# Sorted expert pairs visited in the order of ranks 0, 3, 1, 4, 2, 5, the lighter ranks cut to 64 slots, the rare pass's condition moved to the second pair

## The chip, the cores and the metric

The kernel runs on one core of a Trainium2 chip. The metric is the device time of one execution in microseconds; below it is given as the median of a few executions, and beside it stands one execution that was taken with the hardware profiler. PE is TensorE, DVE is VectorE, ACT is ScalarE, POOL is GpSimd, SP is the engine that issues the transfers.

## The reference

Two networks follow each other on 256 tokens of width 1024: a block with two feed-forward parts and a mixer, and then two layers that each end in a mixture of experts. The change touches only the mixture:

```python
def grouped_moe(h, w_router, router_bias, w_gate, w_up, w_down):
    scores = jax.nn.sigmoid((t @ w_router).astype(jnp.float32))
    # best 1 of 4 groups by the sum of its two best experts, then the best 2 experts in it
    combine = (one_hot(eidx, N_EXPERTS) * w[..., None]).sum(-2)
    for e in range(N_EXPERTS):                       # 16 experts of width 512
        he = jax.nn.silu(t @ w_gate[e]) * (t @ w_up[e])
        y = y + combine[:, e:e + 1] * (he @ w_down[e])
```

Every token goes to two of the 16 experts, so an expert sees some 32 tokens on average, and how many it really sees depends on the data.

## The kernel before, in words

`moe` (L1741) runs once per layer, after `route` has found the experts. It walks over eight **pairs** of experts. A pair owns twelve weight tiles of 1 MB: eight of gate and up, four of down. Sixteen tiles fit on the chip at a time, and `pump` (L316 and after) issues a tile's transfer on SP as soon as the tile 16 places earlier has been released: eight places free after a pair's gate and up (`self.release(8)`), four after its down. Each transfer raises one of eight semaphores in turn and first waits for the transfer eight places before it, so at most eight are under way.

Two pairs (`FIXED = 2`) stand in the order of the weights. The other six are sorted by `sort` (L1406): the count of a pair is that of its fuller expert, `pick` is a matrix that says which pair stands at which place, and SP reads the sorted numbers into registers, from which the later transfers take their addresses. Places p = 2 to 7 so hold ranks 0 to 5, fullest first.

How much a pair computes depends on its count `cv`, by branches that are taken on the chip:

- every pair: gate and up for slots 0 to 31 (`gate_up`, L1582, on `x(0)`), the activation (`swiglu`), down, and the scatter of the pair before it into the result `xT`;
- `cv > 32`: gate and up for slots 32 to 63 (in `more_gate_up`, L1626), and the longer `down2` (L1611) for both;
- `cv > 64`: slots 64 to 95 as well. Their tokens are gathered by `over_pick` and `over_turn`, ahead of knowing whether they are needed, in the `cv > 32` branch. `downs` then has a further branch (L1652), and `more_scatter` (L1754) adds their rows behind the next pair;
- `cv > 96`: the **rare pass** (`rest`, L1728), one condition for the whole layer, `top > NORMAL`. It stands at p = 3 (`RARE_AT`), and its body, which fetches weights once more into the pages that `gather` also uses, is skipped here.

At odd p below 7 a `gather` (L1466) collects the tokens of the next two pairs: PE multiplies one-hot rows by the hidden state into PSUM, and ACT and DVE copy the result into two pages, from which the next pair's `x(0)` is read.

A pair below is **light** when it runs slots 0 to 31 alone, **middle** with the `cv > 32` branch, **heavy** with the `cv > 64` branch.

Of the kernel before, what the change touches and what calls it, by code (L numbers as in the profile page):

```python
# [11 lines left out]
F32 = mybir.dt.float32  # L12
# [4 lines left out]
ALU = mybir.AluOpType  # L17
AX = mybir.AxisListType
ENG = mybir.EngineType

P = 128
S = 256
# [169 lines left out]
def _consts():  # L192
    t = np.arange(P)
    iota = np.broadcast_to(np.arange(1, 257, dtype=np.float32), (P, 256))
    tri = (t[:, None] < t[None, :]).astype(np.float32)
    i4 = np.arange(4)
    before = np.broadcast_to((i4[None, :] < i4[:, None]).astype(np.float32).reshape(1, 16), (P, 16))
    ip = np.arange(NPAIR - 2)
    ahead = np.broadcast_to((ip[None, :] < ip[:, None]).astype(np.float32).reshape(1, -1), (P, ip.size ** 2))
    inv = np.broadcast_to((10000.0 ** (-np.arange(16) / 16)).astype(np.float32), (P, 16))  # L200
    seg = np.broadcast_to((np.arange(256) % 64 != 0).astype(np.float32), (P, 256))
    parts = [("ident", np.eye(P, dtype=np.float32)), ("iota", iota), ("tri", tri), ("before", before),
             ("ahead", ahead), ("inv", inv), ("seg", seg)]
    off = 0
    for n, a in parts:
        _CO[n] = (off, a.shape[1])
        off += a.shape[1]
    return np.ascontiguousarray(np.concatenate([a for _, a in parts], axis=1).astype(np.float32))


FIXED = 2
NDYN = NPAIR - FIXED
NORMAL = 96
LAST = 224
RARE_AT = 3
LEVELS = (64, 32, 16, 8, 4, 2, 1, 0)


# [52 lines left out]
class K:  # L271
# [1137 lines left out]
    def sort(self, cnt, comb):  # L1409
        v = self.nc.vector  # L1410
        n = NDYN
        w0 = self.taken
        t = lambda w, nm, dt=F32: self.rt.tile([P, w], dt, name=self.uid(nm), tag=nm)
        sq = lambda x: x[:, :].rearrange("p (i j) -> p i j", i=n)
        c = cnt[:, FIXED:NPAIR]
        a, b = c.unsqueeze(1).to_broadcast([P, n, n]), c.unsqueeze(2).to_broadcast([P, n, n])
        gt, ge, tm = t(n * n, "ogt"), t(n * n, "oge"), t(2 * n * n, "otm")
        v.tensor_tensor(sq(gt), a, b, ALU.is_gt)
        v.tensor_tensor(sq(ge), a, b, ALU.is_ge)
        v.copy_predicated(gt, self.ahd, ge)  # L1420
        rk = t(n, "ork")
        v.tensor_reduce(rk, sq(gt), AX.X, ALU.add)
        io = self.co("iota")[:, 0:n]
        v.scalar_tensor_tensor(sq(ge), rk[:, :].unsqueeze(1).to_broadcast([P, n, n]), 1.0,
                               io.unsqueeze(2).to_broadcast([P, n, n]), ALU.add, ALU.is_equal)
        pick = sq(ge)
        out = []
        for src, nm in ((self.posm, "posp"), (comb, "comp")):
            dst = t(32, nm)
            for tt in range(2):  # L1430
                o = tt * 16
                v.tensor_copy(dst[:, o:o + 2 * FIXED], src[:, o:o + 2 * FIXED])
                tm4 = tm[:, :].rearrange("p (q e j) -> p q e j", q=n, e=2)
                dims = [P, n, 2, n]
                e2 = src[:, o + 2 * FIXED:o + 16].rearrange("p (j e) -> p e j", e=2)
                v.tensor_tensor(tm4, e2.unsqueeze(1).to_broadcast(dims), pick.unsqueeze(2).to_broadcast(dims), ALU.mult)
                v.tensor_reduce(dst[:, o + 2 * FIXED:o + 16], tm[:, :].rearrange("p (a b) -> p a b", b=n), AX.X, ALU.add)
            out.append(dst)
        self.posm, self.comb = out
        srt = t(2 * n + 1, "srt")  # L1440
        for k, src in enumerate((c, io)):
            v.tensor_tensor(sq(gt), src.unsqueeze(1).to_broadcast([P, n, n]), pick, ALU.mult)
            v.tensor_reduce(srt[:, k * n:(k + 1) * n], sq(gt), AX.X, ALU.add)
        v.tensor_scalar(srt[:, n:2 * n], srt[:, n:2 * n], 12.0, float(w0 + 12 * (FIXED - 1)), ALU.mult, ALU.add)
        v.tensor_reduce(srt[:, 2 * n:], cnt, AX.X, ALU.max)
        self.srti = t(2 * n + 1, "srti", I32)
        v.tensor_copy(self.srti, srt)
        for q in range(n):
            r = self.nc.values_load(self.srti[0:1, n + q:n + q + 1], engines=[ENG.SP], min_val=w0,
                                    max_val=w0 + 12 * NPAIR - 12)  # L1450
            for i in range(12):
                self.dyn[w0 + 12 * (FIXED + q) + i] = r + i
# [173 lines left out]
    def more_gate_up(self, p, cv, gu, x1, tg, h2, pw):  # L1626
        nc, tc = self.nc, self.tc
        ox = self.rt.tile([P, 2, S], F32, name=self.uid("ox"), tag="ox")
        with tc.If(cv > 32):
            xs = self.over_pick(p, 64)  # L1630
            ps = self.mm()
            last = self.gate_up(ps, gu, x1, range(4))
            last = self.chain(last, self.over_turn(xs, ox))
            self.weigh(pw, p, 0, 1)
            last = self.gate_up(ps, gu, x1, range(4, 8), last)
            nc.scalar.activation(tg, ps, AF.Copy)
            with tc.issue_after(last.ins):
                with tc.If(cv > 64):
                    ps = self.mm()
                    self.gate_up(ps, gu, lambda k, e: ox[:, k // 4, (k % 4) * 64 + 32 * e:(k % 4) * 64 + 32 * e + 32])  # L1640
                    t2 = self.sq512()
                    nc.scalar.activation(t2, ps, AF.Copy)
                    self.swiglu(t2, h2)

    def downs(self, p, cv, dn, hT, y, w, more):
        nc, tc = self.nc, self.tc
        pss = [self.mm() for _ in range(2)]
        with tc.If(cv > 32) as c:
            last = self.down2(pss, dn, hT[0], hT[1])
            self.y_page(y, pss, w)  # L1650
            with tc.issue_after(last.ins):
                with tc.If(cv > 64):  # L1652
                    w2, st2 = more[2:]
                    pw = self.tmp.tile([P, 2, P], F32, name=self.uid("pw"), tag="t1")
                    ps2 = [self.acc() for _ in range(2)]
                    last = self.down(ps2, dn, hT[2])
                    with tc.issue_after(last.ins):
                        self.weigh(pw, p, 64)
                        self.slot_w(pw, w2, st2)
                    self.y_page(more[:2], ps2, w2)  # L1660
        with c.Else():
            self.down(pss, dn, hT[0])
            self.y_page(y, pss, w)

    def rare(self, p, e, lo, w0):
        nc = self.nc
# [61 lines left out]
    def rest(self, w0):  # L1728
        engs = [ENG.PE, ENG.Activation, ENG.DVE, ENG.SP]
        load = lambda i: self.count(i, engs)  # L1730
        top = self.nc.values_load(self.srti[0:1, 2 * NDYN:2 * NDYN + 1], engines=engs, min_val=0, max_val=S)
        with self.tc.If(top > NORMAL):
            for p in range(NPAIR):
                cv = load(p)
                for lo in (NORMAL, LAST):
                    with self.tc.If(cv > lo):
                        for e in range(2):
                            self.rare(p, e, lo, w0)

    def moe(self, l, ahead):  # L1740
        nc = self.nc  # L1741
        v = nc.vector
        self.l = l
        self.route(l)
        engs = [ENG.PE, ENG.Activation, ENG.DVE]
        w0 = self.taken
        self.pump()
        tg = [self.rt.tile([P, 512], F32, name=self.uid("tg"), tag=f"tg{i}") for i in range(2)]
# [3 lines left out]
        more = [self.rt.tile([P, D], F32R, name=self.uid("y2"), tag=f"y2{i}") for i in range(2)]  # L1752
        more += self.slots("st2")

        def more_scatter():
            with self.tc.If(cvp > 64):
                self.scatter(more[0], more[1], more[3])

        for p in range(NPAIR):
            base = (p % 2) * P  # L1760
            pw = self.rt.tile([P, 2, P], F32, name=self.uid("pw"), tag="pw")
            self.weigh(pw, p, 0)
            gu = [[[self.get(nm) for _ in range(2)] for nm in ("w_gate_2", "w_up_2")] for _ in range(2)]
            x = lambda lvl: lambda k, e: xe[k // 4][:, (k % 4) * S + base + 64 * e + 32 * lvl:
                                                    (k % 4) * S + base + 64 * e + 32 * lvl + 32]
            hT = [self.rt.tile([P, S], F32, name=self.uid("hT"), tag=f"hT{i}") for i in range(3)]
            ps = self.mm()
            last = self.gate_up(ps, gu, x(0))
# [3 lines left out]
                self.more_gate_up(p, cv, gu, x(1), tg[1], hT[2], pw)  # L1772
            gu = None
            self.release(8)
            if p > 0:
                more_scatter()
            w, st = self.slots("sT", 2)
            self.slot_w(pw, w, st)
            last = None
            if prev is not None:  # L1780
                self.scatter(*prev, 0, 4)
            if p == RARE_AT:
                self.rest(w0)
            for i in range(2):
                self.swiglu(tg[i], hT[i])
            if prev is not None:
                last = self.scatter(*prev, 4, 4, 512)
            if p % 2 == 1 and p < NPAIR - 1:
# [9 lines left out]
            prev, cvp = (y[0], y[1], st), cv  # L1798
            dn = None
            self.release(4)  # L1800
        more_scatter()
        if l == 1:
            self.final_diag()
        self.scatter(*prev)
# [208 lines left out]
```

## Time and profile before

| | us |
|---|---|
| median of 3 executions (1515.75 to 1520.26) | 1518.95 |
| the profiled execution's own time | 1516.88 |
| its span | 1515.1 |
| PE busy (share of the span) | 1373.0 (91%) |
| DVE busy | 971.5 (64%) |
| ACT busy | 683.5 (45%) |
| transfers of the weights' queue, as a share of 16 engines' span | 67.2% |

The page divides the span by engine. The two mixtures are the stretches from about 745 to 1018 us and from about 1255 to 1504 us. The rows below are read from there: a timeline row gives start, duration, engine, line, operation, tile written and tiles read, the count of instructions merged, and in brackets the idle time before it with what ended that. A window row gives busy time by engine, the clock that TensorE was granted (1.00 is 2.4 GHz, 0.50 is 1.2 GHz), the busy share of the DMA engines and what they moved.

### The profile page before, as it was taken

Reading aid. Unit: us, or ns where it says so; the run is one execution under the profiler, and the core shown is the slowest. Engines: PE = TensorE matmul, PEld = TensorE weight load, DVE = VectorE, ACT = ScalarE, POOL = GpSimd, SP = SyncE. Lnnn points to the kernel's source line nnn. Section 1 sums busy time; section 2 is a strip of 40 time slices with the busy share of each in tenths; the row PEclk is TensorE's granted clock in tenths of the full one; section 3 lists DMA queues with packets and bytes.
Section 4 is the critical chain, followed back from the end, with each engine's and each line's share of the span. In section 5 each row is a group of like instructions: output and inputs, shape, how many; then the busy total and the mean of one; then the engine's idle time right before and its main releaser. Section 6 shows DMA issues by size and latency. Waiting matters only on the chain. (4 is left out here: it accounts for less than half of the span.)

```text
span 1515.1 us, 27586 instructions
## 1 busy us (share of the span) xinstructions
PE 1373.0 (91%) x10666; PEld 1091.1 (72%) x10666; DVE 971.5 (64%) x2159; ACT 683.5 (45%) x1466; POOL 72.5 (5%) x86
## 2 busy tenths in 40 slices
PE   7999999989999999999878988668999988897986
PEld 7999998889999987999633344238889985234344
DVE  7999677888888788877531234248888764133243
ACT  7565458665555677555321112136755542011121
POOL 2010000010000003000000000000020010000001
PEclk9999999999999999999998989969999998998998
DMA  9777335378786042695599658963419786988794
GB/s 376 310 317 305 142 107 186 112 303 330 299 333 255 18 182 84 252 372 219 218 420 394 275 243 341 418 261 107 175 71 395 262 328 258 412 332 324 328 412 191
DMA packets 56909, 404.06 MB, mean 267 GB/s; under 512 B 6432, under 2 KB 6560, under 8 KB 8992
## 3 DMA queue, kind: packets, MB, share of 16 engines
q1 hardware_dynamic: 56736, 401.73, 67.2%
q8 instruction: 112, 1.84, 0.5%
q14 instruction: 61, 0.50, 0.1%
HBM read 400.66 MB, written 1.05 MB: 265 GB/s over the span
## 5 line engine op out<-in xcount | busy, mean ns | idle before, releaser
L385 ACT ACTIVATE whi<-w 128x512 fp32r<-128x512 f32 (+3 forms) x438 | 309.0, 737 | 241.8 <-PE mm L403 143.5
L386 DVE TENSOR_TENSOR wlo<-w,whi 128x512 fp32r<-128x512 f32 (+3 forms) x438 | 354.1, 829 | 62.5 <-ACT whi L385 61.3
L402 PE MATMUL mm<-nh,whi 128*128 128x256 f32 x1312 | 372.5, 284 | 14.3 <-ACT whi L385 13.6
L404 PE MATMUL mm<-nh,wlo 128*128 128x256 f32 x1312 | 369.9, 282 | 4.6 <-DVE wlo L386 4.5
L403 PE MATMUL mm<-nl,whi 128*128 128x256 f32 x1312 | 369.4, 282 | 0.3 <-DVE nl L525 0.2
L402 PEld LDWEIGHTS mm<-nh,whi 128*128 128x128 f32 x1312 | 248.9, 190 | 16.6 <-ACT whi L385 14.1
L404 PEld LDWEIGHTS mm<-nh,wlo 128*128 128x128 f32 x1312 | 248.5, 189 | 7.0 <-DVE wlo L386 6.3
L403 PEld LDWEIGHTS mm<-nl,whi 128*128 128x128 f32 x1312 | 248.8, 190 | 1.8 <-DVE nl L525 0.7
L1586 PE MATMUL mm<-w,pg 128*32 128x512 f32 x1472 | 191.7, 622 | 23.8 <-DMA w<-in_w_dram 22.1
L1586 PEld LDWEIGHTS mm<-w,pg 128*32 128x32 f32 x1472 | 52.1, 113 | 148.4 <-issue 104.7
L495 DVE SCALAR_TENSOR_TENSOR ada<-w,cact,ada 128x512 f32<-128x512 f32 x168 | 128.2, 763 | 6.8 <-ACT ada L492 3.5
L402 PE MATMUL acc<-hh,whi 128*128 128x256 f32 x352 | 98.9, 283 | 1.0 <-ACT whi L385 1.0
L403 PE MATMUL acc<-hl,whi 128*128 128x256 f32 x352 | 99.1, 282 | 0.0
L404 PE MATMUL acc<-hh,wlo 128*128 128x256 f32 x352 | 99.1, 282 | 0.0
L1529 DVE SCALAR_TENSOR_TENSOR xTt<-acc,mod,xTt 128x256 f32<-128x256 f32 x152 | 64.1, 476 | 42.8 <-PE acc L1526 42.7
L1535 DVE SCALAR_TENSOR_TENSOR pg<-mm,sm,pg 128x512 fp32r<-128x512 f32 x32 | 24.0, 750 | 71.6 <-ACT pg L1534 53.0
L402 PEld LDWEIGHTS acc<-hh,whi 128*128 128x128 f32 x352 | 66.8, 190 | 1.1 <-ACT whi L385 1.1
L403 PEld LDWEIGHTS acc<-hl,whi 128*128 128x128 f32 x352 | 67.0, 190 | 0.0
L404 PEld LDWEIGHTS acc<-hh,wlo 128*128 128x128 f32 x352 | 67.0, 191 | 0.0
L1549 DVE TENSOR_TENSOR ox<-acc,sm 128x256 f32<-128x256 f32 x14 | 5.3, 420 | 90.6 <-PE acc L1576 90.6
L1534 ACT ACTIVATE pg<-mm,sm 128x512 fp32r<-128x512 f32 x32 | 22.0, 688 | 82.6 <-PE mm L1608 51.6
L403 PE MATMUL mm<-wlo,nh 128*128 128x512 f32 (+2 forms) x144 | 53.5, 372 | 5.9 <-DVE wlo L386 5.9
(422 smaller groups left out, 2342.9 us busy)
## 6 DMA issues: line engine op xcount, KB each, us to landing
w<-in_w_dram SPq DMA_DIRECT2D x371, 1024.0 KB, 9.2
w<-in_w_dram SPq DMA_DIRECT2D x4, 832.0 KB, 8.7
w<-in_w_dram SPq DMA_DIRECT2D x4, 576.0 KB, 3.8
xTt<-in_xT_dram SPq DMA_DIRECT2D x2, 512.0 KB, 6.0
w<-in_w_dram SPq DMA_DIRECT2D x2, 512.0 KB, 7.3
mT<-in_memT_dram SPq DMA_DIRECT2D x1, 1024.0 KB, 17.3
bias<-in_alibi_dram SPq DMA_DIRECT2D x1, 1024.0 KB, 5.3
out_dram<-nl SPq DMA_DIRECT2D x4, 256.0 KB, 3.1
```

The costliest lines, as they stand in the source:

```text
L385: a = self.nc.scalar.activation(hi[:, c], ap[:, c], AF.Copy)
L386: d = self.nc.vector.tensor_tensor(lo[:, c], ap[:, c], hi[:, c].bitcast(F32), ALU.subtract)
L402: mm(ps, lhsT=l[0], rhs=r[0], start=start, stop=False)
L403: mm(ps, lhsT=l[0], rhs=r[1], start=False, stop=False)
L404: mm(ps, lhsT=l[1], rhs=r[0], start=False, stop=stop)
L495: nc.vector.scalar_tensor_tensor(a, raw[:, k * 512:(k + 1) * 512], self.cact[:, 4 * h + k:4 * h + k + 1], a, ALU.mult, ALU.add)
L1529: nc.vector.scalar_tensor_tensor(self.xT[:, k], ps[:, i * S:(i + 1) * S], self.mod[:, self.l, 40 + k:41 + k], self.xT[:, k], ALU.mult, ALU ...
L1534: self.nc.scalar.activation(yh, ps, AF.Copy, scale=w)
L1535: self.nc.vector.scalar_tensor_tensor(yl, ps, w, yh.bitcast(F32), ALU.mult, ALU.subtract)
L1549: v.tensor_tensor(x3, pt, self.G2[:, 4 * h:4 * h + 4].unsqueeze(2).to_broadcast(dims), ALU.mult)
L1586: last = self.chain(last, self.nc.tensor.matmul(ps[32 * g:32 * g + 32, :], lhsT=x(k, e), rhs=gu[k // 4][w][e][:, (k % 4) * 512:(k % 4 + 1) ...
```

## The change

Three edits. The sorted places hold ranks 0, 3, 1, 4, 2, 5 instead of 0 to 5. Ranks 3 to 5 (at p = 3, 5 and 7) lose the code for slots 64 to 95: no picked rows, no inner branches, no `more_scatter` behind them; should such a pair have more than 64, the rare pass takes them, so its condition now also looks at the count of these ranks plus 32. And the rare pass stands at p = 1, behind the two activations, instead of at p = 3 ahead of them.

```diff
 FIXED = 2
 NDYN = NPAIR - FIXED
+RANKS = (0, 3, 1, 4, 2, 5)
+LIMITS = tuple([96] * FIXED + [96 if r < 3 else 64 for r in RANKS])
 NORMAL = 96
-LAST = 224
-RARE_AT = 3
+HALF = 64
+RARE_AT = 1
...
-        v.scalar_tensor_tensor(sq(ge), rk[:, :].unsqueeze(1).to_broadcast([P, n, n]), 1.0,
-                               io.unsqueeze(2).to_broadcast([P, n, n]), ALU.add, ALU.is_equal)
+        v.tensor_tensor(sq(ge), rk[:, :].unsqueeze(1).to_broadcast([P, n, n]),
+                        self.co("rank").unsqueeze(2).to_broadcast([P, n, n]), ALU.is_equal)
...
-        v.tensor_reduce(srt[:, 2 * n:], cnt, AX.X, ALU.max)
+        top = srt[:, 2 * n + 1:3 * n + 2]
+        v.tensor_tensor(top[:, 1:], srt[:, 0:n], self.co("spare"), ALU.add)
+        v.tensor_reduce(top[:, 0:1], cnt[:, 0:FIXED], AX.X, ALU.max)
+        v.tensor_reduce(srt[:, 2 * n:2 * n + 1], top, AX.X, ALU.max)
...
+        more = LIMITS[p] > HALF
         with tc.If(cv > 32):
-            xs = self.over_pick(p, 64)
+            if more:
+                xs = self.over_pick(p, 64)
             ps = self.mm()
             last = self.gate_up(ps, gu, x1, range(4))
-            last = self.chain(last, self.over_turn(xs, ox))
+            if more:
+                last = self.chain(last, self.over_turn(xs, ox))
             self.weigh(pw, p, 0, 1)
             last = self.gate_up(ps, gu, x1, range(4, 8), last)
             nc.scalar.activation(tg, ps, AF.Copy)
+            if not more:
+                return
...
-                for lo in (NORMAL, LAST):
+                for lo in (LIMITS[p], LIMITS[p] + P):
...
-            if p > 0:
+            if p > 0 and LIMITS[p - 1] > HALF:
                 more_scatter()
...
+            for i in range(2):
+                self.swiglu(tg[i], hT[i])
             if p == RARE_AT:
                 self.rest(w0)
-            for i in range(2):
-                self.swiglu(tg[i], hT[i])
...
-        more_scatter()
+        if LIMITS[-1] > HALF:
+            more_scatter()
```

In `downs` the branch for slots 64 to 95 is likewise built only where `LIMITS[p] > HALF`; two small constant rows, `rank` and `spare`, are added to the constants.

**SP, first layer, second pair.** Tiles w174 to w185 are the third pair's weights, w186 to w189 the first four of the fourth pair's. Before, they stand in a row (the ISA rows compute addresses, the branch rows between them only mark where a branch of the other engines joins):

```order
L342 DMA w184_9857<-in_w_dram 128x2048 [waits DMAHW2_49,PE_49]
L342 ISA
L342 DMA w185_9859<-in_w_dram 128x2048 [waits DMAHW3_49,PE_49]
L342 ISA
L342 DMA w186_10086<-in_w_dram 128x2048 [waits DMAHW4_49,PE_49]
```

With the change the rare pass's branch stands between w185 and w186, and where it joins again SP waits for all eight transfer semaphores:

```order
L346 DMA w184_9859<-in_w_dram 128x2048 [waits DMAHW2_49,PE_49]
L346 ISA
L346 DMA w185_9861<-in_w_dram 128x2048 [waits DMAHW3_49,PE_49]
L1749 COMPARE_AND_BRANCH
```

```order
L1749 UNCONDITIONAL_BRANCH
L1749 UNCONDITIONAL_BRANCH [waits SP_sequencer_49,DMAHW0_49,DMAHW1_49,DMAHW2_49,DMAHW3_49,DMAHW4_49,DMAHW5_49,DMAHW6_49,DMAHW7_49]
L1660 UNCONDITIONAL_BRANCH
L346 ISA
L346 DMA w186_14862<-in_w_dram 128x2048 [waits DMAHW4_49,PE_49]
```

The branch moved past 24 transfers: before, it stood behind w209, the last of the fifth pair's.

**ACT, first layer, second pair.** Behind the activations (`sg`) stand the four copies of the gather into the pages (`pg`) that the third pair reads. Before:

```order
L1598 ACTIVATE sg_1287_9917<-acc_1286_9912 128x256 [waits DVE_49,PE_49]
L1598 ACTIVATE sg_1289_9925<-acc_1288_9920 128x256 [waits DVE_49,PE_49,Activation_49]
L1483 ACTIVATE pg_1293_9945<-acc_1295_9947,mod_97,sm_1092_8269 128x256 [waits PE_49]
L1483 ACTIVATE pg_1293_9945<-acc_1296_9958,mod_97,sm_1092_8269 128x256 [waits PE_49]
L1483 ACTIVATE pg_1294_9946<-acc_1297_9969,mod_97,sm_1092_8269 128x256 [waits PE_49]
```

With the change:

```order
L1749 UNCONDITIONAL_BRANCH
L1749 UNCONDITIONAL_BRANCH [waits Activation_49,Activation_sequencer_49]
L1490 ACTIVATE pg_2637_14721<-acc_2639_14723,mod_97,sm_1092_8269 128x256 [waits DMAHW4_49,DMAHW2_49,DMAHW6_49,DMAHW0_49,PE_49]
L1490 ACTIVATE pg_2637_14721<-acc_2640_14734,mod_97,sm_1092_8269 128x256 [waits PE_49]
L1490 ACTIVATE pg_2638_14722<-acc_2641_14745,mod_97,sm_1092_8269 128x256 [waits DMAHW5_49,DMAHW3_49,DMAHW7_49,DMAHW1_49,PE_49]
```

The waits on transfers came with the rare pass, whose body writes these pages by transfer; before, the gather at p = 3 carried them.

## Rows read from the trace of the kernel before

**Rows 1.** Windows of 10 us in the first layer's mixture (all engines, clock, DMA).
```profile
780.00:790.00 10.00, 10.00 (x91) 6.60 (x93) 6.81 (x16) 4.40 (x8) 0.00 (x0) 1.00 1.01 417
...
850.00:860.00 10.00, 10.00 (x91) 3.19 (x94) 1.42 (x4) 0.59 (x1) 0.00 (x0) 1.00 0.18 73
...
890.00:900.00 10.00, 10.00 (x98) 2.97 (x93) 3.78 (x9) 2.71 (x6) 0.00 (x0) 1.00 0.23 79
```
**Rows 2.** ACT at L1642 (heavy pairs only), L1636 (middle and heavy): all, then timeline.
```profile
L1642 ACT ACTIVATE sq<-mm x3: 597/597/597, 821.9 to 1328.2; 128x512 f32<-128x512 f32 x3
...
L1636 ACT ACTIVATE tg<-mm x7: 592/597/597, 823.6 to 1439.3; 128x512 f32<-128x512 f32 x7
...
864.90 0.60 ACT L1642 ACTIVATE sq<-mm 128x512 f32<-128x512 f32 x1 [14.11 <-PE mm L1586]
...
914.55 0.60 ACT L1636 ACTIVATE tg<-mm 128x512 f32<-128x512 f32 x1 [7.16 <-PE mm L1586]
```
**Rows 3.** Timeline of PE, first layer, p = 1 to the last down.
```profile
765.03 7.70 PE L1586 MATMUL mm<-w,pg 128*32 128x512 f32 x64
...
788.66 4.45 PE L1586 MATMUL mm<-w,pg 128*32 128x512 f32 x34
...
799.07 6.04 PE L1586 MATMUL mm<-w,pg 128*32 128x512 f32 x28 [1.08 <-DMA w<-in_w_dram]
805.04 0.50 PE L1555 MATMUL acc<-nh,pm 128*128 128x512 f32 x1
...
840.21 7.91 PE L1586 MATMUL mm<-w,pg 128*32 128x512 f32 x66
...
896.81 7.91 PE L1586 MATMUL mm<-w,pg 128*32 128x512 f32 x66
...
930.30 7.07 PE L1586 MATMUL mm<-w,pg 128*32 128x512 f32 x64 [0.46 <-PEq L1652]
...
950.16 4.03 PE L1586 MATMUL mm<-w,pg 128*32 128x512 f32 x31
...
1003.54 6.20 PE L1608 MATMUL mm<-w,hT 128*32 128x512 f32 x28 [4.49 <-issue]
```
**Rows 4.** Around the rare pass's skipped branch: PE, ACT in both layers, the branch itself.
```profile
878.42 1.94 PE L1594 MATMUL acc<-cot,tg 128*128 128x128 f32 x8 [6.60 <-PEq L1732]
...
885.83 1.93 ACT L1483 ACTIVATE pg<-acc,mod,sm 128x256 f32<-128x256 f32 x4 [4.99 <-SPq L1732]
...
1387.94 1.93 ACT L1483 ACTIVATE pg<-acc,mod,sm 128x256 f32<-128x256 f32 x4 [9.90 <-SPq L1732]
...
L1732 PEldq COMPARE_BRANCH  x2: 5889/6377/6865, 871.1 to 1368.6; - x2
```
**Rows 5.** Timeline of PE, second layer, p = 2 to the last down.
```profile
1306.49 4.92 PE L1586 MATMUL mm<-w,pg 128*32 128x512 f32 x28 [0.58 <-DMA w<-in_w_dram]
1311.34 0.50 PE L1555 MATMUL acc<-nh,pm 128*128 128x512 f32 x1
...
1345.67 7.91 PE L1586 MATMUL mm<-w,pg 128*32 128x512 f32 x66
...
1391.35 7.88 PE L1586 MATMUL mm<-w,pg 128*32 128x512 f32 x66 [0.56 <-PEq L1652]
...
1421.57 7.91 PE L1586 MATMUL mm<-w,pg 128*32 128x512 f32 x66 [0.68 <-PEq L1652]
...
1455.41 7.07 PE L1586 MATMUL mm<-w,pg 128*32 128x512 f32 x64 [0.56 <-DMA w<-in_w_dram]
...
1494.56 3.64 PE L1608 MATMUL mm<-w,hT 128*32 128x512 f32 x32 [0.86 <-DVE xTt L1529]
```
**Rows 6.** Timeline of PE, the last pair's scatter, both layers.
```profile
1013.87 0.55 PE L1525 MATMUL acc<-sT,pg 128*128 128x256 f32 x1 [4.13 <-DVEq L1756]
...
1499.96 0.35 PE L1525 MATMUL acc<-sT,pg 128*128 128x256 f32 x1 [1.76 <-DVEq L1756]
```
**Rows 7.** Timeline of DVE, one small operation of the sort.
```profile
744.36 0.14 DVE L1445 TENSOR_REDUCE srt<-sm 128x1 f32<-128x8 f32 x1
```

More of the change, by code (lines that the diff above doesn't have):

```diff
@@ L199, in _consts @@
     ahead = np.broadcast_to((ip[None, :] < ip[:, None]).astype(np.float32).reshape(1, -1), (P, ip.size ** 2))
+    spare = np.broadcast_to(np.array([NORMAL - x for x in LIMITS[FIXED:]], np.float32), (P, NDYN))
+    rank = np.broadcast_to(np.array(RANKS, np.float32), (P, NDYN))
     inv = np.broadcast_to((10000.0 ** (-np.arange(16) / 16)).astype(np.float32), (P, 16))
@@ L202, in _consts @@
     parts = [("ident", np.eye(P, dtype=np.float32)), ("iota", iota), ("tri", tri), ("before", before),
-             ("ahead", ahead), ("inv", inv), ("seg", seg)]
+             ("ahead", ahead), ("rank", rank), ("spare", spare), ("inv", inv), ("seg", seg)]
     off = 0
@@ L1439, in sort @@
         self.posm, self.comb = out
-        srt = t(2 * n + 1, "srt")
+        srt = t(3 * n + 2, "srt")
         for k, src in enumerate((c, io)):
@@ L1444, in sort @@
         v.tensor_scalar(srt[:, n:2 * n], srt[:, n:2 * n], 12.0, float(w0 + 12 * (FIXED - 1)), ALU.mult, ALU.add)
-        v.tensor_reduce(srt[:, 2 * n:], cnt, AX.X, ALU.max)
+        top = srt[:, 2 * n + 1:3 * n + 2]
+        v.tensor_tensor(top[:, 1:], srt[:, 0:n], self.co("spare"), ALU.add)
+        v.tensor_reduce(top[:, 0:1], cnt[:, 0:FIXED], AX.X, ALU.max)
+        v.tensor_reduce(srt[:, 2 * n:2 * n + 1], top, AX.X, ALU.max)
         self.srti = t(2 * n + 1, "srti", I32)
-        v.tensor_copy(self.srti, srt)
+        v.tensor_copy(self.srti, srt[:, 0:2 * n + 1])
         for q in range(n):
@@ L1650, in downs @@
             self.y_page(y, pss, w)
[L1651 to L1660, printed above, removed]
+            if LIMITS[p] > HALF:
+                with tc.issue_after(last.ins):
+                    with tc.If(cv > 64):
+                        self.more_down(p, dn, hT, more)
         with c.Else():
@@ L1663, in downs, with more_down @@
             self.y_page(y, pss, w)
+    def more_down(self, p, dn, hT, more):
+        w2, st2 = more[2:]
+        pw = self.tmp.tile([P, 2, P], F32, name=self.uid("pw"), tag="t1")
+        ps2 = [self.acc() for _ in range(2)]
+        last = self.down(ps2, dn, hT[2])
+        with self.tc.issue_after(last.ins):
+            self.weigh(pw, p, 64)
+            self.slot_w(pw, w2, st2)
+        self.y_page(more[:2], ps2, w2)
     def rare(self, p, e, lo, w0):
@@ L1730, in rest @@
         load = lambda i: self.count(i, engs)
-        top = self.nc.values_load(self.srti[0:1, 2 * NDYN:2 * NDYN + 1], engines=engs, min_val=0, max_val=S)
+        top = self.nc.values_load(self.srti[0:1, 2 * NDYN:2 * NDYN + 1], engines=engs, min_val=0,
+                                  max_val=S + NORMAL - HALF)
         with self.tc.If(top > NORMAL):
```

## The prediction

> **What bounds the kernel now.** I read the windows first, then the two timelines of PE, then the waits. In the mixtures PE and the queue of weights take turns at being the limit. In the window from 780 us the DMA share is 1.01 at 417 GB/s, so a tile of 128x2048 f32 (1.05 MB) takes 2.5 us; in the windows from 850 and 890 us it is 0.18 and 0.23 [rows 1]. Those two windows alone leave 10 x (0.82 + 0.77) = 16 us of transfer time unused. Why: which branches ran is seen from ACT. The copy that only heavy pairs have ran three times in both layers, the last at 1328.2; the one of middle and heavy pairs seven times [rows 2]. So the six sorted pairs were heavy, heavy, middle, light, light, light in the first layer and heavy, middle, middle, middle, light, light in the second. The heavy ones stand together and keep all sixteen places full while the queue rests; the light ones stand at the end. The timeline of PE [rows 3] prices a place from one gate and up to the next: the heavy pair at p = 2 takes 840.21 - 805.04 = 35.2 after its gate and up, the heavy one at p = 3, with the rare pass's branch and a gather, 896.81 - 840.21 = 56.6, the light one at p = 5 930.30 to 950.16 = 19.9. The last two light ones together take 950.16 to the end of the last down, 1003.54 + 6.20 = 1009.74: 59.6 us, that is 60 us of transfers for their 24 tiles. There the queue is the limit. A pair shorter than 30 us needs tiles that came while a longer one ran: that is what the new order touches.
>
> **The order, first layer.** It becomes heavy, light, heavy, light, middle, light. An even middle pair after a heavy one takes 930.30 - 896.81 = 33.5 [rows 3], after a middle one 1421.57 - 1391.35 = 30.2 [rows 5]. The 3.3 between them are the rows for slots 64 to 95 of the pair before; I add them to whatever follows a heavy pair. But first the third pair has to begin.
>
> **The rare pass, moved to p = 1.** Its body is skipped before and after, but its place is not free. Rows 4 show what it costs at p = 3: PE's branch takes 5.9 to 6.9 us and PE waits 6.60 for it; ACT's four gather copies, behind it, wait 4.99 us in the first layer and 9.90 us in the second for SP's end of the branch. They wait because the skipped body would write the pages that they write, and SP's end of the branch waits for all eight transfer semaphores, that is for every transfer under way. At p = 3 SP had little left in flight. At p = 1 the queue is saturated [rows 1]: the branch stands behind w185, the third pair's last tile, so the copies wait until that tile is there, and the third pair's gate and up reads the pages. Before, that gate and up began at 788.66 and ended with the queue: it waited last for DMA at 799.07 (its eighth tile, w181) [rows 3]. w185 is four tiles later: 799.07 + 4 x 2.5 = 809.1; the copies come at some 0.5 each (1.93 for four [rows 4], on two engines), so PE starts at 809.6 where it started at 788.66. In the second layer the same wait for DMA ended at 1306.49 [rows 5], so w185's counterpart lands at 1316.5 and PE starts near 1317.
>
> How fast does it then run? 64 matmuls took 7.07 us at 930.30, 0.110 each; after an idle time of 4.49 us 28 matmuls took 6.20, which is 0.221 each, the lower clock; 28 behind a wait for a tile took 6.04 [rows 3]. After an idle time three times as long I take 29 at 0.221 and 35 at 0.110: 10.3 us. The Trainium skill, "TensorE: Matmul & The Clock Gate", Part 1, has the clock throttled by default and released only by activity, which speaks against making PE stop here; by it the restart costs 10.3, without it 7.07, and the trace's two cold groups agree. So gate and up end at 819.9 instead of 805.04 (+15), and at 1327.4 instead of the 1311.34 at which the pick began [rows 5] (+16). PE's own branch of 6 us is covered by this wait; without the wait it would show. SP passes no transfer late otherwise: sixteen places are full until p = 1's down frees four. What DVE and ACT have queued behind the copies (the second pair's outputs, then scattered behind the third's gate and up) is late too; some of it may show, 0 to 4 us, counted at nothing.
>
> **Sum, first layer.** 819.9 + 35.2 (heavy) = 855.1; light at p = 3, 19.9 + 3.3 = 878.3; heavy at p = 4, 7.07 + 35.2 = 920.5; light 23.2 = 943.7; middle 30.2 = 973.9; light 19.9 = 993.8, against 1009.74: **-16**. From 809 the remaining 60 tiles need 150 us, so 959, and 35 us of rest still fit before 994. Bounds: -20 if the restart is warm and the outputs don't show, -11 if the light pairs find one tile in five late.
>
> **Sum, second layer.** It becomes heavy, middle, middle, light, middle, light. 1327.4 + 1345.67 - 1311.34 (34.3) = 1361.7; an odd middle took 1455.41 - 1421.57 = 33.8, plus 3.3 after the heavy one, less what it no longer picks for slots 64 to 95 (0 to 3.6, the last being a whole gather, 33.8 - 30.2; I take 2, as it is about half of one): 35.1, at 1396.8; middle 30.2 = 1427.0; light 19.9 = 1446.9. These two take 50 us where 24 tiles take 60, so p = 6 waits 0 to 10; I take 5. Then 30.2 and 19.9: 1502.0, against 1494.56 + 3.64 = 1498.20 [rows 5]: **+4**, between -3 and +8. Here the rare pass's old place gave back 45.7 - 33.8 = 11.9 (the middle pair at p = 3 took 1391.35 - 1345.67), less than the +16 at the new one.
>
> **Small things.** The last scatter waited 4.13 and 1.76 us for the branch of `more_scatter` [rows 6], which is gone behind the last pair: -4.5, with a microsecond of the two waits kept for what is late next (the last outputs). The inner branches that go (PE waits of 0.46 to 0.68 [rows 3, 5]) and the two `more_scatter` branches behind p = 3 and 5: -1. The sort gets two more small operations of 0.14 us [rows 7] ahead of the registers, in both layers: +0.4 with what lies between. The two constant rows ride in a transfer that is made anyway: nothing.
>
> **The number.** -16 + 4 - 4.5 - 1 + 0.4 = -17. From the profiled execution's 1516.88 that is 1499.9; the median of before lies 2.1 above that execution, so **1502**. About 0.3%, 4.6 us, is what a measurement of this kernel can tell from none.
>
> **Rivals.**
> - *The order gives nothing and the moved wait remains (slower).* The transfers that the light pairs lack come late anyway, as SP stands at p = 1 until the queue is empty and starts it again from nothing. Each layer then pays +16 and has back what the branch cost at p = 3, 4.99 and 9.90 [rows 4]: +8.5 on the mean, and -4.5 of the tails: 2 x 8.5 - 4.5 = +12, to 1531. It decides where the two idle windows [rows 1] don't shrink: each us of rest that stays is a us not gained. For it: the second layer's sum, already above zero. Against: three light pairs at 59.6 for two [rows 3] show a lack of transfers behind 16 us of rest. Chance 0.14.
> - *No change.* A light pair at an odd place with a gather cost 788.66 - 765.03 = 23.6 at p = 1 [rows 3], not 19.9. All the new light ones but none of the old stand at odd places: 3.7 x 3 in the first layer and 3.7 x 1 in the second (its last one has no gather) eat 15 of the 17: 1517. Against: 19.9 was itself taken at p = 5, a place with a gather. Chance 0.16.
> - *The branch doesn't hold the copies at p = 1.* If the tiles' semaphores are read as of the branch's start, the third pair begins when it did: no +15 and +16, and only PE's 6 us at each place; 1502 - 31 + 2 = 1473. Against: ACT's waits of 4.99 and 9.90 [rows 4]. Chance 0.06.
> - *Shorter jumps.* The 4.49 us without a releaser ahead of 1003.54 [rows 3] stand in a light pair, behind branches that jump over the bodies for more slots; with the bodies of three ranks shortened such stalls may shrink. If three of five light pairs had back 2 to 3 us: -8, to 1494. For it: that row alone. The Trainium skill, "Runtime: NRT & Kernel Launch", section "Instruction fetch mechanics", says that a taken branch to a target outside the two pages held forces a fetch before execution goes on; no row here shows pages. Chance 0.08.
> - *It doesn't do what it says.* A rank of 3 or more above 64 would set off the rare pass. Excluded: the heavy copies ran three times, in ranks 0 and 1 of the first layer and rank 0 of the second [rows 2].
>
> **How the numbers follow.** The forecast, -8 to -25, has 0.56. Faster: 0.56 + 0.06 + 0.08 = 0.70; same 0.16; slower 0.14. The range reaches from the colder bounds of the sums and the shorter jumps, 1487, to past the case of no change, 1521 (+4, the worse ends of both layers); it leaves out the slower rival and the branch that doesn't hold, 0.2.
>
> **What would show it.** In the changed profile ACT's first copy of the gather at p = 1 waits 10 to 15 us for SP's end of the branch, until about 809 and 1317; the third pair's gate and up ends near 820 and 1328, a first part at the lower clock; the last downs end near 994 and, shifted by the first layer's gain, 1486; the waits of 4.13 and 1.76 are gone, and no window of the first mixture behind p = 3 stays at 0.2 of DMA for 10 us. Wrong would be: a third pair that begins before 800 (the branch doesn't hold), a light pair at p = 3 or 5 above 27 us, or a wait for tiles at p = 4 in the first layer (the queue never recovered).

## The result and the profile after

| | before | after |
|---|---|---|
| median, us | 1518.51 | 1502.57 |
| profiled execution's span, us | 1515.1 | 1501.1 |
| PE busy, us | 1373.0 | 1367.6 |
| first mixture, first gate and up to the last down | 261.8 | 243.2 |
| from there to the second mixture's first gate and up | 246.0 | 248.2 |
| second mixture, the same stretch as the first | 242.5 | 247.1 |
| from its last down to the end of the span | 16.9 | 15.9 |

The changed kernel takes 0.9897 of the time before (95% interval 0.9875 to 0.9919). The five stretches of the two spans, with the start of the first mixture 1.2 us earlier, add up to the 14.0 us between them, but for rounding: -1.2 - 18.6 + 2.3 + 4.6 - 1.0. The second layer loses a quarter of what the first gains. The experiments show that the 16 us between the medians are what is left of larger terms: with the rare pass's branch placed where it costs least, order and cut gain some 40, and the place of the branch costs some 8 in the kernel before and some 32 in the changed one.

The timeline of PE in the changed kernel, first layer, answers to [rows 3] (starts of p = 2 to 7 and the last down):

```profile
809.87 10.04 PE L1593 MATMUL mm<-w,pg 128*32 128x512 f32 x66 [9.71 <-ACT pg L1490]
819.85 0.50 PE L1562 MATMUL acc<-nh,pm 128*128 128x512 f32 x1
...
853.82 1.90 PE L1593 MATMUL mm<-w,pg 128*32 128x512 f32 x10
...
878.65 7.89 PE L1593 MATMUL mm<-w,pg 128*32 128x512 f32 x66
...
921.00 1.04 PE L1593 MATMUL mm<-w,pg 128*32 128x512 f32 x2
...
943.76 7.89 PE L1593 MATMUL mm<-w,pg 128*32 128x512 f32 x66
...
973.27 1.05 PE L1593 MATMUL mm<-w,pg 128*32 128x512 f32 x2 [0.46 <-PEq L1665]
...
985.33 4.60 PE L1615 MATMUL mm<-w,hT 128*32 128x512 f32 x32
```

The same view of the second layer, where [rows 5] stood before:

```profile
1301.33 10.07 PE L1593 MATMUL mm<-w,pg 128*32 128x512 f32 x66 [9.89 <-ACT pg L1490]
...
1345.32 1.90 PE L1593 MATMUL mm<-w,pg 128*32 128x512 f32 x10
...
1380.56 7.89 PE L1593 MATMUL mm<-w,pg 128*32 128x512 f32 x66
...
1410.07 8.26 PE L1593 MATMUL mm<-w,pg 128*32 128x512 f32 x64 [0.46 <-PEq L1665]
...
1431.88 3.66 PE L1593 MATMUL mm<-w,pg 128*32 128x512 f32 x28 [1.36 <-DMA w<-in_w_dram]
1439.39 1.92 PE L1593 MATMUL mm<-w,pg 128*32 128x512 f32 x4 [3.85 <-DMA w<-in_w_dram]
...
1481.13 4.14 PE L1615 MATMUL mm<-w,hT 128*32 128x512 f32 x32
```

Why the third pair starts at 809.87 and 1301.33 stands in the timeline of ACT; the four copies of the gather were held by SP's end of the skipped branch:

```profile
809.25 1.93 ACT L1490 ACTIVATE pg<-acc,mod,sm 128x256 f32<-128x256 f32 x4 [30.12 <-SPq L1749]
...
1300.71 1.93 ACT L1490 ACTIVATE pg<-acc,mod,sm 128x256 f32<-128x256 f32 x4 [29.99 <-SPq L1749]
```

And the windows show what the order gave back; before, the windows from 850 and 890 us had a DMA share of 0.18 and 0.23 [rows 1]:

```profile
820.00:830.00 10.00, 10.00 (x82) 3.89 (x86) 1.42 (x4) 1.18 (x2) 0.00 (x0) 1.00 0.14 56
...
850.00:860.00 10.00, 7.91 (x61) 3.61 (x54) 4.51 (x10) 2.31 (x5) 0.00 (x0) 0.93 0.97 383
...
890.00:900.00 10.00, 10.00 (x94) 3.07 (x90) 1.42 (x4) 0.00 (x0) 0.00 (x0) 1.00 0.94 389
```

The one rest that stays lies behind the third pair's late start (820 to 830), where all places are full: SP waits 21.0 us there for PE to release one.

### The profile page after: what moved, and what is told of

It is laid out like the page before. It is cut to its first block, busy times and chain, and to the rows that moved or that the text cites. A ratio compares the mean times of both kernels' runs of the same rounds, so it can differ in the third digit from the quotient of the medians.

```text
span 1501.1 us, 27480 instructions
## 1 busy us (share of the span) xinstructions
PE 1367.6 (91%) x10654; PEld 1090.7 (73%) x10654; DVE 969.4 (65%) x2157; ACT 680.7 (45%) x1464; POOL 72.6 (5%) x86
## 5 line engine op out<-in xcount | busy, mean ns | idle before, releaser
L406 PE MATMUL mm<-nh,whi 128*128 128x256 f32 x1312 | 373.4, 285 | 14.3 <-ACT whi L389 13.5
L406 PEld LDWEIGHTS mm<-nh,whi 128*128 128x128 f32 x1312 | 249.7, 190 | 16.6 <-ACT whi L389 14.1
L1593 PE MATMUL mm<-w,pg 128*32 128x512 f32 x1472 | 184.5, 616 | 27.2 <-ACT pg L1490 19.6
L1510 DVE TENSOR_TENSOR pw<-cot,posp 128x128 f32<-128x128 f32 x52 | 12.9, 286 | 70.3 <-PE acc L1521 70.2
L1490 ACT ACTIVATE pg<-acc,mod,sm 128x256 f32<-128x256 f32 x32 | 17.4, 564 | 87.3 <-SPq L1749 60.1
```

Of the source, the lines that this page charges most:

```text
L406: mm(ps, lhsT=l[0], rhs=r[0], start=start, stop=False)
L1490: nc.scalar.activation(o, ps[:, :S], AF.Identity, bias=sh, scale=g)
L1510: self.nc.vector.tensor_tensor(p4, io, b4(self.posm), ALU.is_equal)
L1593: last = self.chain(last, self.nc.tensor.matmul(ps[32 * g:32 * g + 32, :], lhsT=x(k, e), rhs=gu[k // 4][w][e][:, (k % 4) * 512:(k % 4 + 1) ...
```

## The experiments

Theory A is the prediction's: the order gains, and the moved branch takes 15 to 16 us per layer back, through the pages. All times below are medians; each run had the kernel before beside it on the same chip, at 1518.3 to 1519.0.

| run | order | slots of ranks 3 to 5 | rare pass | us | ratio to before (95%) |
|---|---|---|---|---|---|
| before | old | 96 | p = 3 | 1518.5 | |
| after | new | 64 | p = 1 | 1502.6 | 0.9897 (0.9875 to 0.9919) |
| e1 | new | 64 | p = 3 | 1488.9 | 0.9807 (0.9764 to 0.9850) |
| e2 | old | 96 | p = 1 | 1532.0 | 1.0086 (1.0059 to 1.0113) |
| e3 | new | 64 | p = 1, places released behind it | 1470.4 | 0.9688 (0.9658 to 0.9718) |
| e4 | new | 64 | none | 1470.2 | 0.9683 (0.9664 to 0.9703) |
| e8 | new | 64 | p = 1, a page of its own | 1477.5 | 0.9719 (0.9701 to 0.9738) |
| e6 | old | 96 | as e3 | 1509.9 | 0.9935 (0.9913 to 0.9957) |
| e11 | new | 96 | as e3 | 1495.6 | 0.9844 (0.9830 to 0.9857) |
| e15 | old | 64 | as e3 | 1495.9 | 0.9853 (0.9837 to 0.9870) |
| e12 | new | 96, no scatter branch | as e3 | 1479.5 | 0.9746 (0.9729 to 0.9762) |
| e13 | new | bodies short, scatter branch kept | as e3 | 1474.2 | 0.9709 (0.9693 to 0.9726) |
| e14 | new | only the body of down short | as e3 | 1490.5 | 0.9805 (0.9788 to 0.9823) |
| e10 | 0, 4, 1, 5, 2, 3 | 64 | as e3 | 1471.4 | 0.9699 (0.9680 to 0.9718) |

**The two parts of the change apart.** e1 is the changed kernel with the rare pass back in its old place:

```diff
-RARE_AT = 1
+RARE_AT = 3
...
+            if p == RARE_AT:
+                self.rest(w0)
             for i in range(2):
                 self.swiglu(tg[i], hT[i])
-            if p == RARE_AT:
-                self.rest(w0)
```

> Both orders and limits as in the changed kernel, the rare pass back at the fourth pair (p = 3), ahead of the activations. Theory A (the order gives the gain, and the wait for SP's end of the branch at p = 1 takes 15 to 16 us of it back in each layer; a branch at p = 3 costs about 12): the third pair's gate and up ends near 805 and the third place pays some 12, so 1494 to 1503, next to the changed kernel's 1502.6. Theory B (the queue is the limit anyway, so the late third pair costs nothing, and the gain is that the branch left p = 3): 1514 to 1527, next to the kernel before.

e2 is the kernel before with the opposite edit: `RARE_AT = 1`, and the call behind the two `swiglu`.

> The kernel before with only the rare pass moved to p = 1, behind the activations. Theory A: each layer pays 15 to 16 for the late third pair and has back 5 to 12 of the branch at p = 3, so 1523 to 1535, slower than before. Theory B: the move is what gained, 1498 to 1510.

1488.9 and 1532.0: the move costs 1502.6 - 1488.9 = 13.7 with the new order and, against the 1519.0 beside it, 13.0 with the old one. Theory B is out. In e2 the copies of the gather waited 30.14 and 32.85 us for SP's end of the branch, as in the changed kernel. e2 lies in theory A's range. e1 came out below it (1494 to 1503), and the timeline of its PE at p = 3 shows why: in the first layer, at a light pair, the branch costs its own 6.49 and 5.65 more for the copies; in the second, at a middle pair, only the branch shows, as the transfers under way landed while that pair ran.

```profile
858.50 1.94 PE L1601 MATMUL acc<-cot,tg 128*128 128x128 f32 x8 [6.49 <-DVEq L1749]
...
876.51 10.11 PE L1593 MATMUL mm<-w,pg 128*32 128x512 f32 x66 [5.65 <-ACT pg L1490]
...
1353.07 1.94 PE L1601 MATMUL acc<-cot,tg 128*128 128x128 f32 x8 [6.55 <-DVEq L1749]
```

**The place of the branch in SP's order.** e3 keeps the rare pass at p = 1 but lets SP meet it eight tiles earlier:

```diff
             gu = None
-            self.release(8)
+            if p != RARE_AT:
+                self.release(8)
...
             if p == RARE_AT:
                 self.rest(w0)
+                self.release(8)
```

> The changed kernel, with the eight places of the second pair's gate and up released behind the rare pass instead of ahead of it, so that SP meets the branch eight tiles earlier in its order (8 x 2.5 = 20 us earlier). Theory A: the gather's copies no longer wait beyond the time at which they are ready, the third pair begins near 798 and its gate and up ends near 807 to 810 (the queue starts again from empty, 2 to 4 us); 10 to 13 us less in each layer: 1476 to 1484. Theory B: the third pair is earlier but the end is not, 1498 to 1504.

e4 leaves the call of `rest` out:

```diff
-            if p == RARE_AT:
-                self.rest(w0)
```

> The changed kernel without the rare pass: the code for tokens beyond the slots is left out. This is the floor of what placing it can give. Theory A: the third pair's gate and up ends near 805 and 1309 (less the shift), 15 to 16 us per layer: 1468 to 1476. Theory B: 1496 to 1503.

1470.4 and 1470.2: theory B is out here too. e4 lies in theory A's range; e3 is better than its range (1476 to 1484), with 16 us less in each layer where 10 to 13 were expected. In e3 the copies wait for PE alone and the third pair starts from a filled set of tiles at the full clock; its gate and up takes 7.89 us, not 10.04:

```profile
793.95 0.56 ACT L1490 ACTIVATE pg<-acc,mod,sm 128x256 f32<-128x256 f32 x1 [11.05 <-PE acc L1483]
```

```profile
801.59 7.89 PE L1593 MATMUL mm<-w,pg 128*32 128x512 f32 x66
...
866.17 7.89 PE L1593 MATMUL mm<-w,pg 128*32 128x512 f32 x66
```

From the first gate and up to the last down, e3's mixtures take 226.5 and 230.7 us against 243.2 and 247.1 of the changed kernel: 16.6 and 16.4 less, the prediction's +15 and +16 undone. That e3 equals e4 is not quite "free": e4's mixtures take 224.6 and 227.8, 1.9 and 2.9 less, but in its profile the first one began 3.9 us later.

e8 asks whether it is the pages. Only the rare pass's own loads change, SP's stop stays:

```diff
         def load(i, half):
-            t = self.page()
+            t = self.rt.tile([P, 1024], F32, name=self.uid("rp"), tag="rp", bufs=1)
```

> The changed kernel, release order and all, but the rare pass's body loads its weights into a page of its own instead of the gather's pages. SP's end of the branch still waits for w185. Theory A (the third pair was held by ACT's copies through the shared pages): the copies wait for nothing beyond PE, the third pair's gate and up ends near 805 and 1296, 1470 to 1478. Theory E (SP's stop itself holds it: transfers are late behind the branch): 1485 to 1503.

1477.5, inside theory A's range. The copies start at 793.90 and 1272.53, each behind PE, and the third pair's gate and up at 801.1 and 1279.9. So the shared pages carried the wait. It stays 7 us above e3. In its profile, which is 11.0 longer than e3's, 3.2 and 5.5 of them lie in the mixtures (229.8 and 236.2) and 3.6 between the two; SP still stops until w185 has landed, but that this is their cause was not tried.

**Order and slots apart.** With the branch out of the way, four kernels separate the other two edits. e6 is the kernel before with `RARE_AT = 1`, the call behind `swiglu` and the release behind it; e11 is e3 with 96 slots for all:

```diff
-LIMITS = tuple([96] * FIXED + [96 if r < 3 else 64 for r in RANKS])
+LIMITS = tuple([96] * FIXED + [96 for r in RANKS])
```

> The kernel before (ranks 0 to 5 in order, 96 slots everywhere) with the rare pass at p = 1 and the eight places released behind it, where it was seen to cost nothing in the new order. Theory A (order and place add up; the order with its limits is worth some 30 wherever the branch stands): 1470.4 + 30 = 1500, range 1493 to 1508. Theory C (the new order gains only because a short pair stood beside the branch at p = 3; without the branch there the old order is as good): 1470 to 1485.

> The new order with the rare pass placed as in e3_release_behind, but every rank keeps the code for slots 64 to 95, its branches and more_scatter behind the last pair. Theory A (the order carries the gain, the limits are worth the two waits of 4.13 and 1.76 us before the last scatter, one inner branch and what a middle pair picks): 5 to 9 more than that kernel's 1470.4, 1475 to 1480. Theory D (the shorter code of the light ranks carries much of it, by shorter jumps): over 1484.

Both miss theory A, e6 by 2 us (theory C, 1470 to 1485, is far out) and e11 by over 15, where theory D had it. The order alone gives 1509.9 - 1495.6 = 14.3, not 30; the cut to 64 slots gives, in the new order, 1495.6 - 1470.4 = 25.2, not 5 to 9. The waits of PE between 805 and 1012 us (in all, times, longest) show where. First e11:

```profile
PE acc L1532 <- PEq L1637: 4.6, 2, 4.2
PE acc L1532 <- DVEq L1773: 4.1, 1, 4.1
PE acc L1532 <- issue: 4.0, 1, 4.0
PE mm L1615 <- issue: 3.4, 2, 3.2
```

Then the same view of e3, where L1637 is the same branch, `cv > 32`:

```profile
PE acc L1521 <- DVEq L1773: 1.2, 1, 1.2
...
PE acc L1521 <- PEq L1637: 0.5, 3, 0.2
```

A light pair does not run the code for slots 64 to 95 in either kernel. It jumps over it. Where that code is there, PE stands for 2 to 4 us in most light pairs, either at the branch or a little behind it with nothing to wait for. The last pair of the first layer shows two such stops and the restarts at the lower clock after them (29 matmuls in 6.38 us, 0.220 each; the granted clock was 0.50 from 974.0 to 977.0 and from 982.8 to 985.0), and then the scatter's branch, in the timeline of e11's PE:

```profile
974.03 0.37 PE L1532 MATMUL acc<-sT,pg 128*128 128x256 f32 x1 [4.04 <-issue]
...
982.75 6.38 PE L1615 MATMUL mm<-w,hT 128*32 128x512 f32 x29 [3.20 <-issue]
...
993.25 0.55 PE L1532 MATMUL acc<-sT,pg 128*128 128x256 f32 x1 [4.13 <-DVEq L1773]
```

That pair takes 27.6 us from its gate and up to the end of its down in e11 and 16.3 in e3; the light pair at p = 3 takes 26.4 against 22.8, the one at p = 5 of the second layer 23.4 against 19.4. The light pair at p = 5 of the first layer makes no such stop and gains nothing: 22.7 and 22.8. The kernel before had such stops, 4.49 us ahead of 1003.54 [rows 3] and 3.37 ahead of 973.00. Not all of the 25.2 is jumps, though: the one middle pair of rank 3, at p = 3 of the second layer, does run the picks for slots 64 to 95 in e11, and takes 37.3 there against 33.0 in e3.

The trace has a row that bears on what goes on in such a stop. Two of its DMA queues are named "instruction"; on one of them, q8, code comes in pieces of 16 KB (1.85 MB in 113 pieces in e11). Each of e11's two stops, the windows from 970 to 974 and from 979.6 to 982.7 us, holds one such piece (queue, kind: pieces, MB, share of the 16 DMA engines):

```profile
q8 instruction: 1, 0.02, 1.5%
```

```profile
q8 instruction: 1, 0.02, 2.4%
```

The first of them comes and goes between 971.5 and 972.6. The stops of 4.18 us in e11 and of 4.49 and 3.37 before hold one each as well; the wait of 4.13 us for DVE's end of the scatter's branch holds none. So PE stands while a piece of code is brought in, though whose code it is no row says. There are many more pieces than stops, 113 in e11's whole trace and 107 in e3's: most arrive while PE works.

**Is it the length of the jump or the number of branches?** e12, e13 and e14 start from e11, each with one piece of code cut for ranks 3 to 5 (`CUT` is true for them):

```diff
+CUT = tuple([False] * FIXED + [r > 2 for r in RANKS])
...
-            if p > 0 and LIMITS[p - 1] > HALF:
+            if p > 0 and not CUT[p - 1]:
                 more_scatter()
...
-        if LIMITS[-1] > HALF:
+        if not CUT[-1]:
             more_scatter()
```

> The kernel of e11_all_96 (new order, all ranks with the code for slots 64 to 95, 1495.6) without the more_scatter branch behind ranks 3 to 5; what lies in the cv > 32 branches stays, so rows of slots 64 to 95 of those ranks would be left out (there are none in this data). Theory G (what costs is a branch that is executed; for a light pair only this one goes): most of the 25 us between e11_all_96 and e3_release_behind, 1472 to 1482. Theory D (the length of the bodies that a light pair jumps over costs): the waits of 4.1, 3.3 and 1.8 us at this branch go, 7 to 11 less, 1484 to 1489.

e13 keeps that branch and shortens the bodies; e14 makes the second of its two edits alone:

```diff
-        more = LIMITS[p] > HALF
+        more = not CUT[p]
...
-            if LIMITS[p] > HALF:
+            if not CUT[p]:
                 with tc.issue_after(last.ins):
                     with tc.If(cv > 64):
                         self.more_down(p, dn, hT, more)
```

> The kernel of e11_all_96 with the bodies of the cv > 32 branches of ranks 3 to 5 cut (no picked rows, no inner branch in gate and up, none in down: slots 64 to 95 of those ranks are left out, there are none in this data), more_scatter's branches kept. A light pair executes the same branches as in e11_all_96 and only jumps less far. Theory D: 10 to 18 less, 1477 to 1486. Theory G: only the one middle pair of rank 3 gains, 0 to 5 less, 1490 to 1496.

> The kernel of e11_all_96 with only the inner branch of down cut in ranks 3 to 5 (the down of slots 64 to 95 of those ranks is left out, there are none in this data). Theory D: part of e13_short_bodies' gain, 2 to 8 less, 1487 to 1494. Theory G: 1494 to 1497.

e13: 21.4 less than e11, although a light pair executes the very same branches; 4.4 of it lie in the middle pair of rank 3 (32.9 against 37.3). Theory G (the number of branches) is out as the whole cause, and theory D (the distance jumped) fits, with more gain than it said. e14: 5.1 less, within theory D. e12: 16.0 less, within theory G's range (1472 to 1482) and outside theory D's (1484 to 1489). The gains do not add: 16.0 and 21.4 have only 25.2 to share. In the waits of PE between 805 and 1012 us, e13 has lost the stop at `cv > 32` (L1638 there),

```profile
PE acc L1522 <- PEq L1774: 1.2, 1, 1.2
PE acc L1522 <- PEq L1638: 0.8, 3, 0.5
```

while e14, with the long body of gate and up, keeps two of up to 4.5 us, each with a piece of code on q8 in it:

```profile
PE acc L1533 <- PEq L1638: 8.1, 2, 4.5
PE acc L1522 <- PEq L1774: 3.2, 2, 2.2
```

e12, too, keeps that stop (6.0 in two, the longest 4.3), and the pairs of the first layer ahead of which a branch went gain little: 41.3 against 41.8 at p = 4 and 29.6 against 30.3 at p = 6. What gains is the last pair, 16.0 us against 27.6:

```profile
961.49 7.07 PE L1594 MATMUL mm<-w,pg 128*32 128x512 f32 x64 [0.45 <-PEq L1666]
973.51 4.00 PE L1616 MATMUL mm<-w,hT 128*32 128x512 f32 x32 [0.45 <-DVE xTt L1537]
```

Up to the end of its down e12 leaves every branch and every body of this pair as e11 has them, and both of its stops are gone all the same; e12's trace has 113 pieces of code, as many as e11's. So neither the number of branches nor the distance jumped explains it alone. Every cut also moves all the code behind it, and no run moved code without cutting any: whether a jump waits for its piece may hang on where the jump and its target come to lie, and which of the jumps pays was not settled. What is shown is that taking out unused code takes most of the stops away. The Trainium skill, "Runtime: NRT & Kernel Launch", section "Instruction fetch mechanics", says that a taken branch to a target outside the code held on the engine forces a fetch before execution goes on. The trace agrees in that each of these stops of over 3 us holds one transfer of code; no row shows what PE held at a jump.

**Why order and slots need each other.** e15 undoes the order alone, with `RANKS = (0, 1, 2, 3, 4, 5)` in e3:

> The kernel of e3_release_behind with ranks 0 to 5 in their old order: the cut to 64 slots and the rare pass's place stay, only the order is undone. If order and cut add up: 1470.4 + (1509.9 - 1495.6) = 1484.7, range 1479 to 1491. If the cut is what gains and the order does little once light pairs are short (they then lack tiles more, not less, at the end): 1470 to 1476. If the old order hides what the cut gives, since its light pairs wait for tiles: 1496 to 1510.

1495.9, at the edge of the range for its third case: the cut is worth 14.0 in the old order and 25.2 in the new one, and the order 14.3 with the long code and 25.5 with the short. With the three light pairs in a row at the end of the first layer, their stops give way to waits for tiles. The waits of PE between 805 and 1012 us in e15:

```profile
PE mm L1593 <- DMA w<-in_w_dram: 11.1, 7, 3.8
PE mm L1615 <- DMA w<-in_w_dram: 2.7, 2, 1.4
```

e3 has no wait for tiles in that stretch. A pair that gets shorter than its twelve tiles, 30 us at 2.5 each, gains less where several such pairs follow each other.

**Another order.** e10 is e3 with `RANKS = (0, 4, 1, 5, 2, 3)`.

> The kernel of e3_release_behind with ranks in the order 0, 4, 1, 5, 2, 3. In the second layer that makes heavy, light, middle, light, middle, middle, so no pair of 30 us follows two that took 50 us for 24 tiles. Theory A (what is left of waits for tiles in the second layer, 1.4 + 3.8 + 0.6 us at p = 6 and a restart at the lower clock, is the order's): 4 to 9 less, 1461 to 1467. Theory F (the lack of tiles only moves, to p = 4 or 5): 1467 to 1474.

1471.4: no gain over e3's 1470.4. The result lies in theory F's range. The expectation had miscounted: in the second layer p = 6 still follows a middle and a light pair, and the lack of tiles stays there (that pair takes 1385.2 to 1425.8, 40.6 us; in e3 39.2). The best version of the study is e3, 3.1% below the kernel before and 2.1% below the changed one.

## Why the prediction was right, and where its parts were not

The time was right, 1502 against 1502.57, and so was most of the path. That it was right to the microsecond is in part luck: what the order and what the cut are worth were sized wrongly, and the two errors cancelled.

- **The moved branch: right, and shown.** The third pair was to start at 809.6 and end its gate and up at 819.9; it did at 809.87 and 819.85, the first part at the lower clock (granted 0.50 up to 813; 10.04 us in all, 10.3 was forecast). The second layer, shifted by the 17.5 us that its start came earlier, was to end it at 1309.9 and did at 1311.3. e3, e4 and e8 show the cost and the mechanism: 16.6 and 16.4 us, through the shared pages. ACT's wait is 30 us long where 10 to 15 were forecast, since it is counted from its last activation; what it costs is what PE shows.
- **Pair by pair, first layer: right to within 1.3 us until p = 7.** Forecast 855.1, 878.3, 920.5, 943.7 and 973.9; measured 853.8, 878.7, 921.0, 943.8 and 973.3. The last down was to end at 993.8 and did at 985.33 + 4.60 = 989.9: the last light pair took 16.7, not 19.9.
- **Second layer: right.** Forecast, shifted by 17.5: 1344.2, 1379.3, 1409.5, 1429.4, end 1484.5; measured 1345.3, 1380.6, 1410.1, 1429.5, 1485.3. The wait for tiles at p = 6, taken as 5, was 1.36 + 3.85 and 0.57 more.
- **The step that failed: what the cut to 64 slots is worth.** "Small things" gave it 4.5 + 1 us, and 2 in the second layer's middle pair; measured with everything else equal it is 25.2 (e11 to e3). Its counterpart, the order, gives 14.3 without the cut; e6's expectation, from the prediction's terms, had put it at some 30. The sum held because the light pair's price, 19.9, was taken from p = 5 [rows 3], a pair that happened to make no stop. The 23.6 of p = 1 held one, at a skipped `more_scatter`, as the timeline of PE in the kernel before shows:

```profile
776.83 0.66 PE L1514 MATMUL acc<-cot,pw 128*128 128x128 f32 x2 [4.11 <-PEq L1756]
```

  The 59.6 us of the last two light pairs, read as the queue's limit, held 7.9 us of such stops beside 8.9 of waits for tiles; in e15, in the same order with the short code, the two take 51.9. With the long code the three light pairs of the new order's first layer cost 26.4, 22.7 and 27.6 (e11), 76.7 together, near the 77.4 of the rival "no change" (23.2 + 23.2 + 19.9 and three times 3.7); with the short code 22.8, 22.8 and 16.3 (e3), 61.9, where the forecast had 66.3. "Shorter jumps", given a chance of 0.08 and 8 us, named what the sum lacked. How much of the joint gain of 39.5 (e6 to e3) is the cut's depends on which is counted first: either alone gives some 14, and 11 come only with both.
- **The tails: half right.** Behind the second layer 1.0 us came of the 1.76; behind the first, where the wait had been 4.13, nothing did. The waits of [rows 6] are gone in both layers, as the timeline of the changed kernel's PE shows for the last scatters,

```profile
990.71 0.38 PE L1532 MATMUL acc<-sT,pg 128*128 128x256 f32 x1 [0.35 <-ACT pg L1541]
...
1486.05 0.39 PE L1532 MATMUL acc<-sT,pg 128*128 128x256 f32 x1 [0.34 <-ACT pg L1541]
```

  but the whole stretch behind the first layer went from 246.0 to 248.2, and in the other profiled runs it lies between 244.5 and 248.4, whatever the last scatter did.
- **"The order gives nothing"**, the slower rival, comes close to e2: 1532.0, where it had 1531, though 4.5 of its sum were tails that e2 does not touch.

## What to carry to other kernels

A skipped branch can cost at its joint: here SP, joining, waited for every transfer under way, and ACT, which writes pages that the skipped body might write, waited with it for 30 us. In the order of the engine that issues the transfers, place the branch ahead of a batch and not behind it; here that alone was worth 32 us, twice the whole change. Price a pair, or any step with branches, from several of its rows, and if the cheapest and the dearest differ by 4 us at equal work, find out why before using either.

## What the runs showed of the hardware that was not expected

Code that is never run has a price. In most light pairs PE stands 2 to 4.5 us at or behind a jump over a long body, against 0.2 to 0.5 at the same branch over the short one; each of PE's own stops of over 3 us that was looked at here holds one transfer of 16 KB on a queue named "instruction". Behind e11's stops of 4.0 and 3.2 us the granted clock is 0.50, and behind the second a matmul of 128x512 takes 0.22 us instead of 0.11. Three ranks' code for slots 64 to 95, which no token of theirs needed, made up 25 us of 1500, some 4 of them picks that a middle pair did run. The same jumps over the same bodies can stop PE for 7 us in one kernel and not at all in another (the last pair of the first layer, e11 and e12).
